# Another order of the mixer's steps, later memory rows and smaller output chunks in a two-layer encoder kernel

## The chip, the core and the metric

The kernel runs on one core of a Trainium2 chip. The metric is the device time of one execution in microseconds. The runs shown before the change have a median of 2234.5 us (three runs, 2233.97 to 2236.01).

## The reference, cut to what matters

```python
for l in range(2):                                   # x: 256 tokens x 2048, mem: 256 x 2048
    h = rms_norm(x, norm_mix[l])
    g_q, g_k, g_v, g_r, lr_f, lr_b, d_q, d_k, d_v, m_q = split(h @ w_in[l])
    gla = head_norm(gla_fwd + gla_bwd) * silu(g_r)   # gated linear attention, 4 heads
    dil = head_norm(dilated_attention(d_q, d_k, d_v) + relative bias)
    kv  = rms_norm(mem, mem_norm[l]) @ w_mem_kv[l]
    xat = head_norm(softmax(m_q @ km) @ vm)          # memory attention
    x = x + concat(gla, dil, xat) @ w_out[l]
    x = x + square(relu(rms_norm(x, norm_mlp[l]) @ w_up[l])) @ w_down[l]
return rms_norm(x, norm_final)                       # all float32
```

## The kernel before, in words

**Products.** Every weight product goes through `linear` (L192). It makes a 256 x 512 result (two token tiles of 128 x 512 in PSUM, pool `ps_mm`, four buffers, so two products at a time) out of four *quads* of 512 weight rows. A quad's 1 MB is loaded by SyncE (SP) into one of three `raw` buffers (`load_quad`, L182). Both operands are split in a high and a low part: ScalarE (ACT) casts `raw` to `wh` (L203), VectorE (DVE) subtracts to get `wl` (L204, "the cut"), in halves of 512 KB, with four buffers each for `wh` and `wl`, which is two quads. Then TensorE (PE) does 24 matmuls (L221 to L223): 4 slices x 2 token tiles x 3 part products. In a product's last quad they are sorted by token tile. `col(i)` is the product of the normalised input with the i-th 512 columns of `w_in`; `evac` (L228) scales a result and moves it from PSUM into SBUF.

**Two lists of other work.** `turning` holds generators that transpose a 256 x 512 activation on DVE with 16 instructions of 32 x 256 (`turn_blocks`, L102) and then, for `split_turned` (L147), make its high and low parts on ACT and DVE. A tuple such as `(0, 4, 4, 4, 4)` says how many of the 16 each step issues; the step after the tuple makes the parts. `turn(n)` (L162) takes n steps of the first generator in the list, `turn()` empties the list. `linear` calls `turn(1)` once per quad behind the cut. `pending` holds functions of which `linear` calls one per quad (`flush(1)`) behind the quad's matmuls. If a quad needs an input that is not ready, `linear` runs steps of the lists until it is.

**Order.** The program text gives the order of priority; the tile framework (called with `schedule_with_timeline_sim=True`, L802) puts the instructions of each engine in a fixed queue and gives out buffers. `with tc.issue_after(ins)` puts those instructions of the block that run on the engine of `ins` behind it in its queue. Most activations live in one pool, `ring`, of 22 slots of 4 KB per partition (`slot`, L54).

**Start.** Transposed memory (`in_memT`) and the first three quads of `w_mem` are loaded in pieces. Then come two small constants, the four 512 KB chunks of plain memory rows into `x` (L528) and the identity. The memory rows serve only for the memory's row norms: `memory_squares` (L568) squares a chunk on ACT and then loads the input rows over it on GpSimd's (POOL) queue. The steps made by `plan_loads` (L531) load the transposed input `xT` during the values product.

**The mixer of a layer** (from L555): memory keys and values (`w_mem`), column 9 (memory queries `mq`), column 0 (`gq`), column 1 (`gk`), memory attention (`attend_weights` L278, `attend_out` L313), the gates (`log_gates`, L343, 14 slots of the ring; its last result is `gl`), columns 2 and 3 (`gv`), all steps up to `gkT` (L612), the gated-attention weights (`gla_weights`, L395), column 6 (`dq`), the gated output (`gla_out`, L472), column 7 (`dk`), column 4 with its silu gate (`gated(0)`), all turning steps (L633), the dilated attention's weights (L634), column 8 (`dv`), its output, column 5, and then `w_out` in four groups, each with the quads 3, 0, 2, 1 (memory, gated, dilated, gated).

**End.** The last `w_down` group's result is added to `x`, squared with a row sum, and the row norm `rs` made of four partial sums (DVE reduce, two POOL instructions, L79 and L81). Then per token tile two halves of 128 x 1024 are scaled on ACT and DVE (L700 to L706) and stored, 512 KB each (L708).

## Time and profile before

| | |
|---|---|
| median of three runs | 2234.5 us |
| the profiled execution's own time | 2234.38 us |
| its span, first to last instruction | 2232.6 us |
| PE busy | 2195.7 us (98%) |
| DVE busy | 1593.3 us (71%) |
| ACT busy | 1133.5 us (51%) |
| POOL busy | 39.7 us (2%) |
| moved by DMA | 423.27 MB, mean 190 GB/s |
| mean granted clock of PE | 0.996 of 2.4 GHz |

The span is what the profile's times count from; the execution's own time is 1.8 us more, for what lies around it. A row of the timeline gives start and duration in us, engine and line, the operation, result and sources by the program's names, how many instructions were merged in it (x16), and in brackets the idle time of the engine before it with what ended it. The engine names with a q are the queues that issue DMAs.

### The profile page before, as it was taken

The numbers are of one execution on the slowest core, as the hardware profiler recorded it, in microseconds if no ns is written. First come the engines' busy times: TensorE is split into PE (matmuls) and PEld (weight loads), VectorE is DVE, ScalarE is ACT, GpSimd is POOL, SyncE is SP. The second block draws the span as 40 slices with busy tenths as digits, with TensorE's granted clock in tenths as the row PEclk, the third lists the DMA queues.
The fourth block names the chain that finished last, engine by engine and source line by source line (L and its number), as shares of the span: only waits on it lengthen the run. The fifth ranks groups of instructions, "written<-read, shape, count | busy, mean of one in ns | idle before, by whom it ended". The sixth has DMA issues, their size and how long they took to land.

```text
span 2232.6 us, 25769 instructions
## 1 busy us (share of the span) xinstructions
PE 2195.7 (98%) x9898; PEld 1818.4 (81%) x9898; DVE 1593.3 (71%) x2234; ACT 1133.5 (51%) x1529; POOL 39.7 (2%) x69
## 2 busy tenths in 40 slices
PE   7998999999999999999999999999999999999998
PEld 5886888888888888888888878888888888888886
DVE  5658688977577477468986588888765864865774
ACT  7555465554355345345554565655544544543543
POOL 1000000000000000000000000000000000000000
PEclk9999999999999999999999999999999999999999
DMA  9653345555555555555665443555555555555563
GB/s 359 226 172 130 132 151 188 189 192 203 189 190 196 198 188 192 197 196 200 215 202 194 154 158 130 181 189 189 192 202 191 190 194 199 189 189 197 195 211 132
DMA packets 63364, 423.27 MB, mean 190 GB/s; under 512 B 7076, under 2 KB 7844, under 8 KB 14473
## 3 DMA queue, kind: packets, MB, share of 16 engines
q1 hardware_dynamic: 62104, 417.69, 54.6%
q0 software_dynamic: 1136, 3.94, 0.5%
q8 instruction: 77, 1.26, 0.2%
q14 instruction: 47, 0.38, 0.0%
HBM read 419.50 MB, written 3.15 MB: 189 GB/s over the span
## 4 chain that ended last, share of the span: by engine, by line
PE 94%; DVE 2%; DMA 2%; ACT 1%; issue 1%; SPq 0%; POOL 0%; ACTq 0%; POOLq 0%; DVEq 0%
PE mm L222 30%; PE mm L223 30%; PE mm L221 30%; DMA raw<-in_w_mem 1%; PE pv L323 1%; PE go L479 1%; DVE gkT L108 1%; DVE wl L204 0%; PE pT L309 0%; DVE gqT L108 0%; DMA x<-in_mem 0%; DVE dkT0o L108 0%; PE dg L439 0%; ACT junk L93 0%; PE dg L443 0%
## 5 line engine op out<-in xcount | busy, mean ns | idle before, releaser
L204 DVE TENSOR_TENSOR wl<-raw,wh 128x1024 fp32r<-128x1024 f32 (+1 forms) x774 | 928.4, 1215 | 533.0 <-ACT wh L203 528.5
L203 ACT ACTIVATE wh<-raw 128x1024 fp32r<-128x1024 f32 (+1 forms) x774 | 813.6, 1054 | 882.1 <-PE mm L223 824.4
L222 PE MATMUL mm<-wl,uT3h 128*128 128x512 f32 x256 | 99.6, 389 | 0.0
L223 PE MATMUL mm<-wh,uT3h 128*128 128x512 f32 x256 | 99.6, 389 | 0.0
L223 PE MATMUL mm<-wh,zT0h 128*128 128x512 f32 x256 | 99.6, 389 | 0.0
L223 PE MATMUL mm<-wh,uT1h 128*128 128x512 f32 x256 | 99.6, 389 | 0.0
L223 PE MATMUL mm<-wh,zT3h 128*128 128x512 f32 x256 | 99.6, 389 | 0.0
L222 PE MATMUL mm<-wl,zT1h 128*128 128x512 f32 x256 | 99.6, 389 | 0.0
L222 PE MATMUL mm<-wl,uT2h 128*128 128x512 f32 x256 | 99.6, 389 | 0.0
L222 PE MATMUL mm<-wl,zT0h 128*128 128x512 f32 x256 | 99.6, 389 | 0.0
L222 PE MATMUL mm<-wl,uT0h 128*128 128x512 f32 x256 | 99.6, 389 | 0.0
L223 PE MATMUL mm<-wh,uT2h 128*128 128x512 f32 x256 | 99.6, 389 | 0.0
L223 PE MATMUL mm<-wh,uT0h 128*128 128x512 f32 x256 | 99.6, 389 | 0.0
L222 PE MATMUL mm<-wl,uT1h 128*128 128x512 f32 x256 | 99.6, 389 | 0.0
L222 PE MATMUL mm<-wl,zT2h 128*128 128x512 f32 x256 | 99.6, 389 | 0.0
L221 PE MATMUL mm<-wh,zT0l 128*128 128x512 f32 x256 | 99.6, 389 | 0.0
L223 PE MATMUL mm<-wh,zT2h 128*128 128x512 f32 x256 | 99.6, 389 | 0.0
L222 PE MATMUL mm<-wl,zT3h 128*128 128x512 f32 x256 | 99.6, 389 | 0.0
L223 PE MATMUL mm<-wh,zT1h 128*128 128x512 f32 x256 | 99.6, 389 | 0.0
L221 PE MATMUL mm<-wh,uT1l 128*128 128x512 f32 x256 | 99.4, 389 | 0.0
L221 PE MATMUL mm<-wh,zT1l 128*128 128x512 f32 x256 | 99.4, 389 | 0.0
L221 PE MATMUL mm<-wh,uT3l 128*128 128x512 f32 x256 | 99.3, 389 | 0.0
(438 smaller groups left out, 4671.6 us busy)
## 6 DMA issues: line engine op xcount, KB each, us to landing
raw<-in_w_up SPq DMA_DIRECT2D x128, 1024.0 KB, 4.9
raw<-in_w_down SPq DMA_DIRECT2D x128, 1024.0 KB, 4.9
raw<-in_w_in SPq DMA_DIRECT2D x80, 1024.0 KB, 4.9
raw<-in_w_out SPq DMA_DIRECT2D x32, 1024.0 KB, 4.9
raw<-in_w_mem SPq DMA_DIRECT2D x13, 1024.0 KB, 5.5
mem<-in_memT SPq DMA_DIRECT2D x7, 512.0 KB, 6.3
raw<-in_w_mem SPq DMA_DIRECT2D x12, 256.0 KB, 6.0
x<-in_mem SPq DMA_DIRECT2D x4, 512.0 KB, 7.0
```

The source lines that it names most:

```text
L108: yield nc.vector.transpose(dst[f:f + 32, :, :, s:s + 32], src[s:s + 32, :, :, f:f + 32])
L203: nc.scalar.activation(hi, raw[:, k:k + n], AF.Copy)
L204: cut = nc.vector.tensor_tensor(lo, raw[:, k:k + n], hi.bitcast(F32), ALU.subtract)
L221: nc.tensor.matmul(ps[t], xl[:, kk, sl], hi, start=first, stop=False)
L222: nc.tensor.matmul(ps[t], xh[:, kk, sl], lo, start=False, stop=False)
L223: nc.tensor.matmul(ps[t], xh[:, kk, sl], hi, start=False, stop=last)
L323: nc.tensor.matmul(ps[:, h, :], pT[s][:, h, t * P:(t + 1) * P], v[:, s, h * P:(h + 1) * P], start=s == 0, stop=s == NT - 1,)
L479: nc.tensor.matmul(ps[:, j, :], AT[s][:, t, 2 * c + j, :], v[c][:, s, j * DV:(j + 1) * DV], start=s == 0, stop=s == NT - 1,)
```

## The change

Five things are done.

- `linear` gets `late`: the matmuls of the last `late` quads are issued together behind the last one, sorted by token tile. It is 2 for the last `w_down` group of the last layer and 1 elsewhere. What `turn(1)` and `flush(1)` issue on ACT is now put behind the quad's last cast too.
- The memory rows are no longer loaded behind the first weights; `plan_loads` loads one chunk per quad of the values product (`load_rows`).
- The mixer's order: memory attention moves behind column 2 in layer 0 and stays behind column 1 in layer 1; the gates move behind column 2; in layer 1 three turning steps run before column 1; `dq`, `dk` and `mT0` are turned in steps of four with an empty first one; the dilated attention moves behind column 8; `turn()` before it becomes steps until `dk` is ready. The line that appends the turn of `gq` stands twice afterwards: the first is a context line of the diff, the second is added.
- The last group is not added to `x` in the loop but per token tile at the end, and the first three partial sums are reduced ahead of the fourth.
- The output is stored in eight chunks of 256 KB, in the order 0, 3, 2, 1 within a token tile.

```diff
--- before.py
+++ after.py
@@ -189,10 +189,11 @@
             newest[0] = nc.sync.dma_start(raw[:, c * n:(c + 1) * n], wsrc[:, k:k + n, :]).ins
         return raw, pieces
 
-    def linear(wsrc, lhs, quads, loaded=(), pool=ps_mm, tag="mm"):
+    def linear(wsrc, lhs, quads, loaded=(), pool=ps_mm, tag="mm", late=1):
         ps = [pool.tile([P, NW], F32, tag=tag, name=f"mm{t}") for t in range(NT)]
-        nq = len(quads)
+        nq, order = len(quads), []
         for i, q in enumerate(quads):
             raw, n = loaded[i] if i < len(loaded) else load_quad(wsrc, q)
             wh = [wpool.tile([P, 2, NW], F32R, tag="wh", name="wh", bufs=4) for _ in range(2)]
@@ -200,28 +201,31 @@
             n = min(4 // n, 2)
             for k in range(0, 4, n):
                 hi, lo = (w[k // 2][:, k % 2:k % 2 + n] for w in (wh, wl))
-                nc.scalar.activation(hi, raw[:, k:k + n], AF.Copy)
+                cast = nc.scalar.activation(hi, raw[:, k:k + n], AF.Copy)
                 cut = nc.vector.tensor_tensor(lo, raw[:, k:k + n], hi.bitcast(F32), ALU.subtract)
-            with tc.issue_after(cut.ins):
+            with tc.issue_after(cut.ins), tc.issue_after(cast.ins):
                 turn(1)
             while q not in lhs:
                 if pending:
                     flush(1)
                 else:
                     turn(1)
-            xh, xl = lhs[q]
-            order = [(kk, t) for kk in range(4) for t in range(NT)]
+            order += [(i, q, wh, wl, kk, t) for kk in range(4) for t in range(NT)]
+            if nq - late <= i < nq - 1:
+                continue
             if i == nq - 1:
-                order.sort(key=lambda o: o[1])
-            for kk, t in order:
+                order.sort(key=lambda o: o[5])
+            for j, p, wh, wl, kk, t in order:
+                xh, xl = lhs[p]
                 sl = slice(t * P, (t + 1) * P)
-                first = i == 0 and kk == 0
-                last = i == nq - 1 and kk == 3
+                first = j == 0 and kk == 0
+                last = j == nq - 1 and kk == 3
                 hi, lo = wh[kk // 2][:, kk % 2, :], wl[kk // 2][:, kk % 2, :]
                 nc.tensor.matmul(ps[t], xl[:, kk, sl], hi, start=first, stop=False)
                 nc.tensor.matmul(ps[t], xh[:, kk, sl], lo, start=False, stop=False)
                 nc.tensor.matmul(ps[t], xh[:, kk, sl], hi, start=False, stop=last)
-            with tc.issue_after(cut.ins):
+            order = []
+            with tc.issue_after(cut.ins), tc.issue_after(cast.ins):
                 flush(1)
         return ps
 
@@ -524,14 +528,18 @@
     nc.sync.dma_start(rel, a["rel"])
     nc.sync.dma_start(onehot, a["onehot"])
     with tc.issue_after(newest[0]):
-        for c in range(4):
+        nc.sync.dma_start(ident, a["ident"])
+
+    def load_rows(c):
+        with tc.issue_after(newest[0]):
             nc.sync.dma_start(x[:, :, c * NW:(c + 1) * NW], tokens(a["mem"], c))
-        nc.sync.dma_start(ident, a["ident"])
-
-    def plan_loads(name, loads, src, gain, lhs):
+
+    def plan_loads(name, loads, src, gain, lhs, also=None):
 
 
         def step(i):
+            if also is not None and i < 4:
+                also(i)
             for q in loads[i] if i < len(loads) else ():
                 splits[name, q] = split_loaded(
                     slot([4, S], f"{name}{q}"), src, q, gain, f"{name}{q}", lhs
@@ -560,7 +568,7 @@
         if l == 0:
             flush()
             bias_products()
-            plan_loads("x0", ((0, 1), (2,), (3,)), a["xT"], gains[:, 0, 0, :], xlhs)
+            plan_loads("x0", ((0, 1), (2,), (3,)), a["xT"], gains[:, 0, 0, :], xlhs, load_rows)
             ps_v = linear(a["w_mem"][l, 1], mem_lhs, range(4), pool=ps_ax, tag="ax")
             with tc.issue_after(newest[0]):
                 spread_bias()
@@ -598,25 +606,35 @@
             queries_turned()
             gq = evac(col(0), rsq, "gq")
         turning.append(heads_turned(gq, "gqT", heads))
-        ps_gk = col(1)
-        while "mq" not in heads:
-            turn(1)
-        o_mem = attend_out(attend_weights(heads["mq"], heads["km"], None, "mem"), vm, "memo")
-        gk = evac(ps_gk, rs, "gk")
-        gates = log_gates(xlhs, rs, l)
-        turning.append(heads_turned(gk, "gkT", heads))
         mlhs = {}
         mgain = gains[:, 1, l, :]
-        turning.append(split_turned(o_mem, 3, mgain, "mT3", mlhs, (0, 4, 4, 4, 4)))
-        gv = [evac(col(2 + c), rs, f"gv{c}") for c in range(2)]
+
+        def memory_attention():
+            while "mq" not in heads:
+                turn(1)
+            o = attend_out(attend_weights(heads["mq"], heads["km"], None, "mem"), vm, "memo")
+            turning.append(heads_turned(gk, "gkT", heads))
+            turning.append(split_turned(o, 3, mgain, "mT3", mlhs, (0, 4, 4, 4, 4)))
+
+        turning.append(heads_turned(gq, "gqT", heads))
+        if l:
+            turn(3)
+        gk = evac(col(1), rs, "gk")
+        if l:
+            memory_attention()
+        gv = [evac(col(2), rs, "gv0")]
+        if not l:
+            memory_attention()
+        gates = log_gates(xlhs, rs, l)
+        gv.append(evac(col(3), rs, "gv1"))
         while "gkT" not in heads:
             turn(1)
         AT = gla_weights(heads["gqT"], heads["gkT"], gates)
         dq = evac(col(6), rsq, "dq")
         o_gla = gla_out(AT, gv)
-        turning.append(split_turned(dq, "dq", None, f"dqT{l}", heads, (0, 8, 8)))
+        turning.append(split_turned(dq, "dq", None, f"dqT{l}", heads, (0, 4, 4, 4, 4)))
         dk = evac(col(7), rs, "dk")
-        turning.append(split_turned(dk, "dk", None, f"dkT{l}", heads, (0, 8, 8)))
+        turning.append(split_turned(dk, "dk", None, f"dkT{l}", heads, (0, 4, 4, 4, 4)))
 
         def gated(c):
             ps = col(4 + c)
@@ -630,11 +648,11 @@
             mlhs[1] = split_T(o_gla[1], 1, mgain, "mT1")
 
         gated(0)
-        turn()
-        weights = attend_weights(heads["dq"], heads["dk"], bt, "dil")
-        turning.append(split_turned(o_gla[0], 0, mgain, "mT0", mlhs, (4, 4, 4, 4)))
+        turning.append(split_turned(o_gla[0], 0, mgain, "mT0", mlhs, (0, 4, 4, 4, 4)))
         dv = evac(col(8), rs, "dv")
-        o_dil = attend_out(weights, dv, "dilo")
+        while "dk" not in heads:
+            turn(1)
+        o_dil = attend_out(attend_weights(heads["dq"], heads["dk"], bt, "dil"), dv, "dilo")
         turning.append(split_turned(o_dil, 2, mgain, "mT2", mlhs, (0, 4, 4, 4, 4)))
         gated(1)
         pending.append(mixed)
@@ -676,7 +694,10 @@
                     plan_loads(
                         "mem1", ((0,), (1,), (2,), (3,)), a["memT"], gains[:, 3, l + 1, :], mem_lhs
                     )
-                ps = linear(a["w_down"][l, part, g], ulhs, range(up_groups))
+                ending = end and last and g == 3
+                ps = linear(a["w_down"][l, part, g], ulhs, range(up_groups), late=2 if ending else 1)
+                if ending:
+                    continue
                 add_to_x(ps, g)
                 if end and not last:
                     pending.append(lambda g=g: squares_of_x(xnorm, g))
@@ -691,21 +712,25 @@
     out_rows = a["out"].rearrange("(t p) d -> p t d", p=P)
     for t in range(NT):
         v = xchunk(3, t)
+        part = small.tile([P, 1], F32, tag="part", name="part")
+        nc.vector.tensor_reduce(part, fnorm.ssc[:, t, :3], AX.X, ALU.add)
+        nc.gpsimd.tensor_scalar(part, part, 1.0 / D, EPS, ALU.mult, ALU.add)
+        nc.vector.tensor_tensor(v, ps[t], v, ALU.add)
         fnorm.add(3, t, v)
-        rs = fnorm.done(t)
-        for half in (1, 0):
-            for c in (2 * half, 2 * half + 1):
-                v = xchunk(c, t)
-                if c == 3:
-                    nc.vector.scalar_tensor_tensor(
-                        v, v, rs[:, 0:1], fg[1][:, 1, :], ALU.mult, ALU.mult
-                    )
-                elif c == 1:
-                    nc.vector.tensor_scalar(v, v, rs[:, 0:1], None, ALU.mult)
-                else:
-                    nc.scalar.activation(v, v, AF.Copy, scale=rs[:, 0:1])
-            cs = slice(2 * half * NW, (2 * half + 2) * NW)
-            nc.sync.dma_start(out_rows[:, t, cs], x[:, t, cs])
+        m = small.tile([P, 1], F32, tag="m1", name="m_fin")
+        nc.gpsimd.tensor_scalar(m, fnorm.ssc[:, t, 3:], 1.0 / D, part[:, 0:1], ALU.mult, ALU.add)
+        rs = small.tile([P, 1], F32, tag="rs_fin", name="r_fin")
+        nc.gpsimd.tensor_tensor(rs, m, neghalf[:, :1], ALU.pow)
+        for c in (0, 3, 2, 1):
+            v = xchunk(c, t)
+            cs = slice(c * NW, (c + 1) * NW)
+            if c == 3:
+                nc.vector.scalar_tensor_tensor(v, v, rs[:, 0:1], fg[1][:, 1, :], ALU.mult, ALU.mult)
+            elif c == 1:
+                nc.vector.tensor_scalar(v, v, rs[:, 0:1], None, ALU.mult)
+            else:
+                nc.scalar.activation(v, v, AF.Copy, scale=rs[:, 0:1])
+            nc.sync.dma_start(out_rows[:, t, cs], v)
 
 
 def _bucket(rel):
```

## Rows read from the trace of the kernel before

**Rows 1.** The page's first section: busy time, share of the span, instructions per engine

```profile
PE 2195.7 (98%) x9898; PEld 1818.4 (81%) x9898; DVE 1593.3 (71%) x2234; ACT 1133.5 (51%) x1529; POOL 39.7 (2%) x69
```

**Rows 2.** Waits of PE: us in total, times, longest us

```profile
PE mm L222 <- DVE wl L204: 16.3, 6, 9.7
PE mm L221 <- ACT wh L203: 11.0, 4, 5.5
```

**Rows 3.** Stretches: length, each engine's busy time, granted clock, DMA share, GB/s

```profile
10.00:64.50 54.50, 46.72 (x185) 35.24 (x184) 32.16 (x54) 40.07 (x84) 8.54 (x14) 0.97 0.99 374
188.60:207.00 18.40, 8.72 (x35) 6.97 (x34) 17.89 (x37) 6.33 (x17) 0.52 (x1) 0.72 0.18 61
540.00:1080.00 540.00, 540.00 (x2384) 447.16 (x2383) 360.72 (x464) 256.38 (x274) 0.00 (x0) 1.00 0.57 197
```

**Rows 4.** Timeline of SP's DMA issues and of PE, the start

```profile
15.03 2.40 SPq L528 DMA_DIRECT2D x<-in_mem  x4
...
29.10 0.73 PE L221 MATMUL mm<-wh,mem03l 128*128 128x512 f32 x2 [2.53 <-ACT wh L203]
...
64.51 0.61 PE L221 MATMUL mm<-wh,x00l 128*128 128x512 f32 x2
```

**Rows 5.** Timeline of DVE and PE in layer 0, behind the gates

```profile
185.30 1.22 DVE L392 TENSOR_TENSOR gl<-z,gh 128x1024 fp32r<-128x1024 f32 x1
186.44 7.18 DVE L108 STREAM_TRANSPOSE gqT<-gq 32x256 f32<-32x256 f32 x16
193.65 7.20 DVE L108 STREAM_TRANSPOSE gkT<-gk 32x256 f32<-32x256 f32 x16
...
202.76 0.80 PE L222 MATMUL mm<-wl,x00h 128*128 128x512 f32 x1 [9.68 <-DVE wl L204]
```

**Rows 6.** Timeline of ACT, DVE and PE in layer 1, behind the gates

```profile
1292.39 1.24 ACT L231 ACTIVATE gv<-mm,r_mix 128x512 f32<-128x512 f32 x2
1293.65 7.18 DVE L108 STREAM_TRANSPOSE gkT<-gk 32x256 f32<-32x256 f32 x16
...
1302.14 0.50 PE L222 MATMUL mm<-wl,xT0h 128*128 128x512 f32 x1 [1.84 <-DVE wl L204]
```

**Rows 7.** Timeline, layer 0: PE begins columns 7 and 4, evictions between

```profile
226.71 0.39 PE L221 MATMUL mm<-wh,x00l 128*128 128x512 f32 x1
...
237.28 1.28 ACT L231 ACTIVATE dq<-mm,rsq 128x512 f32<-128x512 f32 x2
238.03 0.69 DVE L426 TENSOR_TENSOR qd<-gqT,E 128x512 f32<-128x512 f32 x1
...
255.94 0.39 PE L221 MATMUL mm<-wh,x00l 128*128 128x512 f32 x1
...
280.89 1.25 ACT L231 ACTIVATE dk<-mm,r_mix 128x512 f32<-128x512 f32 x2
```

**Rows 8.** Timeline of PE in layer 0, column 8's first quad

```profile
292.29 0.50 PE L222 MATMUL mm<-wl,x00h 128*128 128x512 f32 x1 [2.74 <-DVE wl L204]
```

**Rows 9.** Timeline of PE and DVE in layer 0: memory attention, third `w_out` quad

```profile
130.47 0.28 PE L236 MATMUL sc<-kmT0h,mqT0l 128*128 128x256 f32 x1
...
158.16 0.67 DVE L337 TENSOR_TENSOR memo<-pv,cmb 128x512 f32<-128x512 f32 x1
...
354.22 1.66 DVE L128 SCALAR_TENSOR_TENSOR mT2l<-mT2o,gains,mT2h 128x256 fp32r<-128x256 f32 x4
...
355.67 0.39 PE L221 MATMUL mm<-wh,mT2l 128*128 128x512 f32 x1
```

**Rows 10.** End: timeline of DVE, SP; DMA issues (KB each, us to landing)

```profile
2220.53 0.69 DVE L502 TENSOR_TENSOR x<-mm,x 128x512 f32<-128x512 f32 x1 [5.84 <-PE mm L223]
...
2224.18 0.68 DVE L502 TENSOR_TENSOR x<-mm,x 128x512 f32<-128x512 f32 x1
...
2223.94 4.57 SPq L708 DMA_DIRECT2D out<-x  x4
...
out<-x SPq DMA_DIRECT2D x4, 512.0 KB, 3.1
```

## The prediction, made before the changed kernel was run

> **What bounds the kernel now.** The page's first section comes first: TensorE (PE) is busy 98% of a span of 2232.6 us, the matmul count is not touched by the change, so all that can be won is PE's idle time, some 37 us, and stretches at the lower clock [rows 1]. Next, PE's waits: in total it waits 16.3 us for VectorE's (DVE) `wl` cuts and 11.0 us for ScalarE's (ACT) `wh` casts; the rest of the idle time is the first 5.5 us and the tail behind the last matmul [rows 2]. Then busy time by stretches: 10 to 64.5 us has PE busy for 46.7 of 54.5 us with the DMA engines at 0.99, 188.6 to 207 us has it busy for 8.7 of 18.4 us at a granted clock of 0.72 with DVE busy for 17.9 us; 540 to 1080 us is unbroken, 2384 matmuls in 540 us, that is 0.2265 us each and 5.44 us for a quad's 24 [rows 3]. So: DMA at the start, DVE in the mixer of layer 0, and a serial tail.
>
> **Part 1, memory rows later.** The four 512 KB loads of memory rows are issued at 15.03 us, ahead of the last `w_mem` quad of the keys; that quad's matmuls end an idle time of 2.53 us at 29.10 us [rows 4]. From the start of that idle time (26.57 us) to the first matmul of column 9 (64.51 us) PE has five quads, 27.2 us of work, and takes 37.9 us: 10.7 us are lost, in six waits for the next weights and in the slower matmuls behind them [rows 3, 4]. The change issues one memory chunk behind each value quad. Everything column 9's first quad needs by then is 2 MB memT, 8 MB weights, 2 MB rows, 2 MB xT and 1 MB of its own; at the stretch's 374 GB/s [rows 3] that is 40 us, and PE reaches it at 53.6 us at best, so the order, not the volume, is what starves PE. The x loads on the GpSimd queue, which now run against the weights since they follow the memory squares, also move behind. What becomes late: the squares of memory and x stand behind a cast in each quad of columns 9 and 0, and casts run at most two quads ahead of PE, so the last squares come near 66 and 88 us and the row norms some 2 us behind them. The evictions that wait for the norms (keys, query) free the PSUM pairs of columns 0 and 1, which PE wants near 53.6 + 4 x 5.44 = 75 and 97 us: 5 us of cover; if that goes, PE waits by the difference. Bounds: all 10.7 us, or half, 5 us, if the weight ring of three raw buffers keeps loads as close as now. I take **-10.0 us**, near the upper end, since PE waits nowhere in 540 us at 197 GB/s, half the start's rate [rows 3].
>
> **Part 2, mixer order.** I counted each transposing step. A `turn(1)` runs per weight quad. The diff appends the turn of `gq` a second time and leaves the first in place, so 16 more DVE transposes (16 take 7.2 us [rows 5]) per layer. More important is the ring of 22 slots. In layer 1 `gkT` starts at 1293.65 us, straight behind the last `gl`, and `gv`, whose matmuls were long done, at 1292.39 us [rows 6]; in layer 0 `gqT` and then `gkT` start only behind the last `gl` (185.30 us) [rows 5]. I read this as slots given out in program order: whatever is traced after the gates waits for the gates' last slot. With the change, layer 0's second `gqT` and `gkT` are still both traced after the gates, so the burst of 32 transposes, 14.4 us, stays, and with it PE's 9.68 us of waiting; layer 1's `gkT` burst of 16 with its 1.84 us stays too [rows 5, 6]. I take **0** (bounds: 7.8 us saved, if only 16 are left as in layer 1; 3 us lost, if the doubled work comes on top). The duplicate itself runs in DVE's gaps.
>
> What moves is the cover. Layer 0's memory attention starts one column later, so one column fewer is left to run beside the gate weights (`gla_weights`). Column 4 needs the PSUM pair of column 6, which the eviction of `dq` frees; that waits in slot order for the second `qd` (238.03 us) and ends at 238.56 us. Column 7's pair is freed by `dk` at 282.14 us, after the gated output [rows 7]. Today column 6 ends near 226.7 us, column 4 starts at 255.9 and column 8 near 289, so neither matters [rows 7, 8]; afterwards column 7 ends where column 6 does in the chain, and PE waits. If the chain were no faster, the waits are 238.6-226.7 less some 3.6 us of chain work, 8 us, and about 11 us more before column 8: 19 us. But PE's queue is then empty of columns, so each chain step starts when ready; with the 4 to 5 us by which the chain's matmuls now stand behind columns taken off, I get 2.5 to 3 us at each place: **+5.2 us** (bounds 0 and 19). The second stall of now, 2.74 us up to 292.29 us for `wl`, goes, since the bunches of eight transposes of `dq` and `dk` before it become fours, spread to the end of column 8: **-2.7 us** [rows 8].
>
> Dilated attention is now traced behind column 8, so column 5 and two `w_out` quads are its whole cover, 10.9 us + 21.8 us + some 10 us of its own and `mT1`'s PE work: 43 us. Its transposed output `mT2`, five turns of which now stand in one row before `w_out`'s third quad, needs the attention (28 us for the memory group, 130.47 to 158.8 us [rows 9]), 7.2 us of transposes, 1.7 us of parts, and what DVE does for others. Today its parts start at 354.22 us, the last of the four ending at 355.88, against a first use at 355.67 us: no slack; layer 1 repeats the pattern [rows 9]. Bounds 0 and 10 us a layer; I take 1.5 us, near the lower, as the transposes may fill DVE's gaps: **+3.0 us**. In layer 1 the gates' loads now stand behind `gv0`'s slot, some 9 us later; `dk` there has about that slack: **+0.4 us**. Putting ACT's parts and squares behind the casts costs nothing in the unbroken stretch: ACT is busy 256 of 540 us there [rows 3].
>
> **Part 3, the tail.** Sorting the last two quads by token tile ends tile 0's sum 2.7 us sooner (12 matmuls). Now tile 0's sum is added at 2220.53 us, tile 1's at 2224.18 us instead of 2.7 us later, because DVE is at tile 0's scalings until then [rows 10]; those 0.9 us go. The reduce of four partial sums (0.16 us and its hand-over) leaves the chain, and the first store needs one scaled chunk rather than two, 0.7 us. Against it stand four more DMA issues of some 0.34 us on SP, of which two lie behind the first store. The stores are then bound by 1 MB at the rate of now (2 MB in four stores, 3.1 us to landing each [rows 10]). I take **-1.4 us** (bounds -2.4 and 0). The Trainium skill, "DMA: Bandwidth & Descriptors", speaks against this step: its section Bandwidth wants transfers of 1 MiB or more, and the fit in "Anatomy of one DMA" (made on transfers issued from GpSimd) has about 2 us of fixed cost in each, an estimate of 2.6 us for 256 KB. By that, four in turn would take 10.4 us against 6.4 us for two of 512 KB. No row here shows them in turn.
>
> **Sum:** -10.0 + 0 + 5.2 - 2.7 + 3.0 + 0.4 - 1.4 = -5.5 us, on the profiled execution's own 2234.38 us (span 2232.6): 2228.9; the median of the runs is 0.1 higher, so **2229.0 us**.
>
> **Rivals.** (a) The mixer gives nothing back: slots are freed early enough, columns never wait for PSUM, `mT2` fits in. For it: the chain steps now stand behind columns. Against: `dq` and `dk` ended exactly in slot order. Time: 2234.5 - 10.0 - 1.4 - 2.7 = 2220.4 us; were the burst halved too, 2212. (b) **Slower:** the PSUM pairs come no earlier than now. Place: columns 4 and 8 of layer 0; price 19 us instead of 5.2, so 2229.0 + 13.8 = 2242.8 us; it decides once `dq` and `dk` gain less than about 4 us each on the chain. For it: evictions and chain are planned beforehand, on estimated times. Against: the planner sees the empty PE. (c) The start gain is not there: with the ring of three raw buffers the rows only move the queue, 5 us instead of 10, hence 2234.0 us, no change. (d) Stores in turn at 3.1 us each instead of overlapping: 6.2 us more than two, 2236.6 us. Against it: the four stores of now are all issued within 4.57 us, overlapping [rows 10]. The Trainium skill's rule above is what would have it so.
>
> **Chances.** Forecast (2225 to 2234) 0.44; (a) 0.22; (b) 0.20; (c) 0.11; (d) 0.03. A measurement of this kernel tells some 0.2%, 4.5 us, from no change. Faster by more: all of (a), 0.6 of the forecast: 0.48. Slower by more: (b) and a rest: 0.22. Within: 0.30. The range takes in most of (a) and (b): 2219 to 2242 us; the forecast's own is 2225 to 2234.
>
> **What would show it.** Start: the first column 9 matmul near 54 us and no wait before it but the first. Burst: 32 transposes in a row behind the last `gl` of layer 0, again. PSUM: two waits of PE of 2 to 4 us, ended by ACT's `dq` and `dk`, and none at the 292 us place. `w_out`: at most 2 us before its third quad in each layer. Tail: tile 1's add within 0.1 us of PE's end, and 8 us from there to the span's end. I am wrong if columns wait longer than 10 us in all in layer 0, if `gqT` and `gkT` are not together behind the gates, or if the start's waits remain.

## The result, and the profile after

The changed kernel takes 2262.65 us (median of four runs, 2257.66 to 2264.41) against 2234.23 us: ratio 1.0119, 95% interval 1.0102 to 1.0136. It is 28.4 us slower, outside the range, and on the other side of the forecast. The profiled execution took 2264.41 us (span 2262.5).

The page's first section answers to [rows 1]: the same 9898 matmuls, PE busy 9.6 us longer although nothing was added to it, and 32 more DVE instructions (16 transposes a layer).

```profile
span 2262.5 us, 25817 instructions
PE 2205.3 (97%) x9898; PEld 1825.8 (81%) x9898; DVE 1608.7 (71%) x2266; ACT 1135.0 (50%) x1529; POOL 41.8 (2%) x71
```

PE's waits after answer to [rows 2]; the columns are the waiting engine and line, the releaser, us in total, times, longest.

```profile
PE mm L224 <- DVE mT0l L128: 18.1, 2, 9.0
PE mm L225 <- DVE wl L205: 13.9, 2, 11.4
PE mm L224 <- ACT wh L204: 6.5, 2, 5.1
PE mm L224 <- ACT dk L235: 5.2, 2, 3.1
PE mm L224 <- DVE mem01l L128: 1.8, 1, 1.8
PE mm L224 <- ACT dq L235: 1.3, 1, 1.3
```

Of the start's waits for `wh` only the first, of 5.1 us, is left (the other in that row, 1.4 us, is in layer 1). New are two waits of 9 us for `mT0l`, one in each layer's `w_out`, and those for `dk` and `dq`. A ledger of the first matmul of each stage, before and after (us from the start of the span), says where the time went:

| first matmul of | before | after | shift | won (-) or lost since the row above |
|---|---|---|---|---|
| column 9, layer 0 | 64.5 | 55.5 | -9.0 | -9.0 |
| `w_out`, layer 0 | 343.9 | 340.7 | -3.1 | +5.9 |
| `w_up`, layer 0 | 431.8 | 442.4 | +10.6 | +13.7 |
| `w_out`, layer 1 | 1438.8 | 1455.4 | +16.6 | +6.0 |
| `w_up`, layer 1 | 1526.7 | 1556.2 | +29.5 | +12.8 |
| end of the span | 2232.6 | 2262.5 | +29.9 | +0.4 |

So the start gave what was forecast, the tail nothing, and each layer lost about 19 us between column 9 and `w_up`. Three places of layer 0 in the timeline show it. First DVE behind the gates (start, duration, engine, line, operation, and in brackets the idle time before with its releaser), which answers to [rows 5]:

```profile
202.32 2.36 DVE L396 TENSOR_TENSOR gl<-z,gh 128x1024 fp32r<-128x1024 f32 x2
204.60 7.18 DVE L108 STREAM_TRANSPOSE gqT<-gq 32x256 f32<-32x256 f32 x16
211.81 7.20 DVE L108 STREAM_TRANSPOSE gkT<-gk 32x256 f32<-32x256 f32 x16
219.04 0.69 DVE L430 TENSOR_TENSOR qd<-gqT,E 128x512 f32<-128x512 f32 x1
```

Against column 9's start, `gl`'s second instruction begins at 148.0 us instead of 120.8, and the burst of 32 is still whole. Then PE's four longest waits in this layer's mixer:

```profile
220.92 0.80 PE L225 MATMUL mm<-wl,x01h 128*128 128x512 f32 x1 [11.43 <-DVE wl L205]
247.23 0.50 PE L224 MATMUL mm<-wh,x00l 128*128 128x512 f32 x1 [1.33 <-ACT dq L235]
288.95 0.80 PE L224 MATMUL mm<-wh,x00l 128*128 128x512 f32 x1 [3.15 <-ACT dk L235]
357.94 0.80 PE L224 MATMUL mm<-wh,mT0l 128*128 128x512 f32 x1 [9.03 <-DVE mT0l L128]
```

And DVE ahead of the last of them, which answers to [rows 9]:

```profile
348.17 0.69 DVE L341 TENSOR_TENSOR dilo<-pv,cmb 128x512 f32<-128x512 f32 x1
348.89 3.12 DVE L108 STREAM_TRANSPOSE mT2o<-dilo 32x256 f32<-32x256 f32 x7
...
355.64 1.34 DVE L108 STREAM_TRANSPOSE mT2o<-dilo 32x256 f32<-32x256 f32 x3
357.01 0.48 DVE L128 SCALAR_TENSOR_TENSOR mT1l<-mT1ps,gains,mT1h 128x256 fp32r<-128x256 f32 x1
357.41 1.66 DVE L128 SCALAR_TENSOR_TENSOR mT0l<-mT0o,gains,mT0h 128x256 fp32r<-128x256 f32 x4
359.11 0.89 DVE L108 STREAM_TRANSPOSE mT2o<-dilo 32x256 f32<-32x256 f32 x2
360.03 0.88 DVE L128 SCALAR_TENSOR_TENSOR mT1l<-mT1ps,gains,mT1h 128x256 fp32r<-128x256 f32 x2
360.82 1.66 DVE L128 SCALAR_TENSOR_TENSOR mT2l<-mT2o,gains,mT2h 128x256 fp32r<-128x256 f32 x4
```

PE waits for `mT0l`, and `mT0l` stands on DVE's queue behind 14 of `mT2`'s transposes. That row invites a theory, and the theory is wrong, as the next section shows. The clock is told by the windows (columns: stretch, length, PE busy and count, granted clock, DMA share, GB/s):

```profile
240.00:245.90 5.90, 5.90 (x34) 1.00 0.53 182
247.20:251.80 4.60, 4.57 (x13) 0.63 0.29 123
251.80:257.00 5.20, 5.20 (x30) 1.00 0.00 0
289.00:293.50 4.50, 4.50 (x14) 0.66 0.02 4
357.94:366.41 8.47, 8.46 (x25) 0.66 0.00 0
366.41:371.90 5.49, 5.49 (x26) 1.00 0.39 122
```

Behind each of these waits the matmuls run partly at the lower level: 24 of them take 8.5 us instead of 5.5 behind the wait of 9.03 us, and 12 take 4.4 and 4.3 us instead of 2.7 behind the two short ones. That is why PE is busier with the count unchanged.

PE's own time closes the account. From column 9 to the `w_up` of layer 1 it takes 38.5 us more (1500.7 instead of 1462.2): it is idle for 26.2 us more (40.5 instead of 14.3) and busy for 12.3 us more with the same 6633 matmuls.

### The profile page after: what moved, and what is told of

The parts are those of the page before. It is cut to its first block, busy times and chain, and to the rows that moved or that the text cites. A ratio compares the mean times of both kernels' runs of the same rounds, so it can differ in the third digit from the quotient of the medians.

```text
span 2262.5 us, 25817 instructions
## 1 busy us (share of the span) xinstructions
PE 2205.3 (97%) x9898; PEld 1825.8 (81%) x9898; DVE 1608.7 (71%) x2266; ACT 1135.0 (50%) x1529; POOL 41.8 (2%) x71
## 3 DMA queue, kind: packets, MB, share of 16 engines
HBM read 419.50 MB, written 3.15 MB: 187 GB/s over the span
## 4 chain that ended last, share of the span: by engine, by line
PE 85%; DVE 2%; ACT 1%; issue 0%; POOL 0%; ACTq 0%; POOLq 0%; DVEq 0%
PE mm L224 28%; PE mm L225 27%; PE mm L226 27%; PE go L483 1%; DVE mT2o L108 1%; DVE wl L205 0%; ACT wh L204 0%; PE pv L327 0%; DVE gkT L108 0%; ACT junk L334 0%; PE pT L313 0%; PE dg L447 0%; PE dg L450 0%; PE xg L470 0%; PE cum L412 0%
```

## The experiments

Every kernel was timed against the kernel before on the same chip. For all of them distances were read in both layers, to and from the start of `dk`'s second eviction (us; "mT2" is the start of the last of its four low parts). The marks are those of the profiled execution; that of e4 took 2258.8 us, 5.4 us more than its median.

| kernel | median | ratio | col. 9 to dk | dk to mT2 | dk to `w_up` | layer 1: `w_up` of layer 0 to dk | dk to `w_up` |
|---|---|---|---|---|---|---|---|
| before | 2234.2 | 1 | 217.0 | 73.9 | 150.3 | 942.2 | 152.7 |
| after | 2262.7 | 1.0119 | 233.3 | 73.2 | 153.6 | 960.9 | 152.9 |
| e1 rows only | 2225.2 | 0.9954 | 217.0 | 74.6 | 151.4 | 942.1 | 152.8 |
| e2 one turn | 2245.0 | 1.0042 | 225.5 | 73.2 | 153.5 | 950.1 | 153.3 |
| e3 mT0 by eights | 2263.5 | 1.0126 | 233.9 | 76.9 | 155.4 | 961.9 | 151.8 |
| e4 attention before col. 8 | 2253.4 | 1.0087 | 233.3 | 74.0 | 151.2 | 962.0 | 148.8 |
| e5 memory attention early | 2253.9 | 1.0085 | 227.7 | 71.7 | 150.7 | 961.8 | 150.8 |
| e6 gates early | 2258.5 | 1.0101 | 228.0 | 73.3 | 153.7 | 952.5 | 164.1 |
| e7 rows and forced tail | 2225.0 | 0.9953 | 216.0 | 74.6 | 151.4 | 942.1 | 152.8 |
| e8 gates early, one turn | 2238.9 | 1.0014 | 215.2 | 73.4 | 152.4 | 945.4 | 164.0 |
| e9 turned before gates | 2230.9 | 0.9976 | 218.0 | 73.3 | 151.4 | 944.8 | 154.1 |
| e10 gates first | 2222.8 | 0.9940 | 218.5 | 72.5 | 148.2 | 944.0 | 151.2 |
| e11 gates, then memory | 2228.6 | 0.9968 | 214.8 | 72.3 | 149.1 | 953.9 | 149.1 |
| e12 three undone | 2230.4 | 0.9982 | 217.9 | 72.5 | 150.4 | 950.1 | 149.3 |
| e13 four undone | 2228.1 | 0.9965 | 214.6 | 74.7 | 151.5 | 944.2 | 154.2 |

The 95% intervals reach 0.0009 to 0.0017 to either side of the ratio.

**The start alone (e1).** The kernel before with `load_rows` and nothing else:

```diff
-        for c in range(4):
-            nc.sync.dma_start(x[:, :, c * NW:(c + 1) * NW], tokens(a["mem"], c))
+    def load_rows(c):
+        with tc.issue_after(newest[0]):
+            nc.sync.dma_start(x[:, :, c * NW:(c + 1) * NW], tokens(a["mem"], c))
...
+            if also is not None and i < 4:
+                also(i)
```

> The kernel before with the later memory rows alone. Theory (the start's gain is real and independent of the rest): column 9's first matmul at 55.5 us as in the changed kernel against 64.5, and the 9.0 us stay to the end, as nothing between there and the end takes up slack: 2234.2 - 9.0 = 2225.2 us, ratio 0.996. Rival (the later squares and x loads are paid for further on, hidden in the changed kernel's other losses): 2229 to 2234 us, with a new wait of PE before column 1 or in the memory attention.

Measured 2225.15 us, ratio 0.9954 (0.9939 to 0.9969). Column 9 starts at 53.8 us, and every later mark keeps the gain (`w_up` of layer 1 1517.1 against 1526.7). The theory holds; so the new mixer lost some 38 us, not 28.

**The doubled turn (e2).** The changed kernel without the first of the two equal lines:

```diff
-        turning.append(heads_turned(gq, "gqT", heads))
```

> The changed kernel without the doubled turn of gq, nothing else. Theory (the bursts behind the gates are what the doubled turn causes): layer 0 has 16 transposes (7.2 us) behind the last gl instead of 32, so PE's 11.4 us wait falls to about 4 us; in layer 1 gkT gets the steps of columns 1 and 2, the 16 behind gl vanish and with them waits of 1.4 and 2.4 us and some slow matmuls. Together 9 to 13 us less than the changed kernel: 2250 to 2254 us. The two waits of 9.0 us before w_out's second quad stay. Rival (the doubled work runs in gaps and the chain behind gl sets the end anyway): 0 to 3 us less, 2260 to 2263 us.

Measured 2244.97 us, 17.7 less than the change as it was, more than expected: the largest single part. In layer 0 the burst is 16 and PE's wait 3.6 us: `gkT` begins straight behind `gl`, at 203.34 us, where as changed (rows above) the second `gqT` stands between them with its 7.2 us.

```profile
203.34 7.17 DVE L108 STREAM_TRANSPOSE gkT<-gk 32x256 f32<-32x256 f32 x16
```

In layer 1 these are DVE's rows, with the one turn and, below them, as changed:

```profile
1257.47 3.56 DVE L108 STREAM_TRANSPOSE gkT<-gk 32x256 f32<-32x256 f32 x8
1262.32 1.79 DVE L108 STREAM_TRANSPOSE gkT<-gk 32x256 f32<-32x256 f32 x4
1267.20 1.80 DVE L108 STREAM_TRANSPOSE gkT<-gk 32x256 f32<-32x256 f32 x4
1303.64 1.23 DVE L396 TENSOR_TENSOR gl<-z,gh 128x1024 fp32r<-128x1024 f32 x1
```

```profile
1266.66 5.36 DVE L108 STREAM_TRANSPOSE gqT<-gq 32x256 f32<-32x256 f32 x12
1273.31 1.79 DVE L108 STREAM_TRANSPOSE gqT<-gq 32x256 f32<-32x256 f32 x4
...
1316.66 1.22 DVE L396 TENSOR_TENSOR gl<-z,gh 128x1024 fp32r<-128x1024 f32 x1
1317.80 7.19 DVE L108 STREAM_TRANSPOSE gkT<-gk 32x256 f32<-32x256 f32 x16
```

There the second turn of `gq` does not cost its 7.2 us of DVE; it takes the steps of the list that `gkT` would have had, and so `gkT` falls behind the gates, where it is in the way. Without it, `gkT` is done 35 us ahead of `gl`. So the duplicate costs its own duration in layer 0 (`dk` 7.9 us later) and another's place in layer 1 (`dk` 10.8 us later). The two waits for `mT0l` stay (17.4 us).

**Where the 9 us in `w_out` come from (e3, e4).** I first held DVE's queue to be the cause: that `mT0`'s parts, tied to the second `w_out` quad, are overtaken by `mT2`'s transposes.

```diff
-        turning.append(split_turned(o_gla[0], 0, mgain, "mT0", mlhs, (0, 4, 4, 4, 4)))
+        turning.append(split_turned(o_gla[0], 0, mgain, "mT0", mlhs, (0, 8, 8)))
```

> The changed kernel with mT0 turned in steps (0, 8, 8) instead of (0, 4, 4, 4, 4), so that its parts belong to column 5's last quad and no longer to w_out's second. Theory (DVE's queue: mT0's low parts stand behind 14 of mT2's transposes, only because their step comes behind the second w_out quad's cut): the two waits of 9.0 us before w_out's second quad vanish, the 2 to 3 us of slow matmuls behind each too, 22 us in all: 2240 to 2243 us; before the third quad at most 2 us of wait in each layer. Rival (the late dilated attention is what costs: mT2 is ready only when it is, and the wait moves to the third quad): waits of 5 to 9 us before w_out's third quad instead, 2255 to 2263 us.

```diff
+        turn()
+        weights = attend_weights(heads["dq"], heads["dk"], bt, "dil")
+        turning.append(split_turned(o_gla[0], 0, mgain, "mT0", mlhs, (4, 4, 4, 4)))
         dv = evac(col(8), rs, "dv")
-        while "dk" not in heads:
-            turn(1)
-        o_dil = attend_out(attend_weights(heads["dq"], heads["dk"], bt, "dil"), dv, "dilo")
+        o_dil = attend_out(weights, dv, "dilo")
```

> The changed kernel with the weights of the dilated attention back before column 8, all steps emptied ahead of it and mT0 in steps (4, 4, 4, 4), as in the kernel before. Theory (DVE's queue): the waits of 9.0 us in w_out vanish as in the run with mT0 by eights, and column 8 has its cover back: 2238 to 2243 us. Rival (late dilated attention): also 2238 to 2243 us here, but only here and not in the run with mT0 by eights. Third possibility (the reordered columns 6, 7, 4 keep costing in some other place): above 2246 us.

With `mT0` by eights, 2263.54 us: nothing won. `mT0l` is ready at 346.9 us, and PE waits one quad later, for `mT2l`. PE's and DVE's rows of that run:

```profile
352.25 0.69 DVE L341 TENSOR_TENSOR dilo<-pv,cmb 128x512 f32<-128x512 f32 x1
353.99 7.17 DVE L108 STREAM_TRANSPOSE mT2o<-dilo 32x256 f32<-32x256 f32 x16
363.12 1.66 DVE L128 SCALAR_TENSOR_TENSOR mT2l<-mT2o,gains,mT2h 128x256 fp32r<-128x256 f32 x4
363.65 0.79 PE L224 MATMUL mm<-wh,mT2l 128*128 128x512 f32 x1 [10.47 <-DVE mT2l L128]
```

My theory fell; the rival had it right that the wait only moves. But the rival's own cause does not hold either: with the attention back ahead of column 8 (2253.43 us, 9.2 less) the long waits in `w_out` go, yet `mT2` is no earlier, its last part starting 74.0 us behind `dk` (73.2 as changed), and `dk` still comes at 233.3 us. The third possibility, above 2246 us, is what happened. In layer 0 of all fifteen kernels `mT2` follows `dk` by 71.7 to 76.9 us and `w_up` follows it by 148 to 155 us. By these marks 35.0 of the 38.5 us lie ahead of `dk`, 16.3 in layer 0 and 18.7 in layer 1; the long waits behind it are where much of that shows.

That distance is no law, though. In the changed order column 8 starts 0.2 us behind `dk`, whose PSUM pair it waits for, and the attention starts some 3 us into column 5 (26.7 us behind `dk`) and takes 33.4 us. With the attention ahead of column 8 it starts 13.0 us behind `dk` and takes 45.3 us beside the column: the two differences nearly cancel. In the kernel before, PE is busy for 147.6 of the 150.4 us from `dk` to `w_up`, so there PE's own work fills the distance; in the changed kernel it is busy for 144.4 of 153.6 us and waits.

**What makes `dk` late (e5, e6, e8).** Layer 0's memory attention back behind column 1; the gates ahead of column 2; and the latter with one turn:

```diff
-        if l:
-            memory_attention()
+        memory_attention()
         gv = [evac(col(2), rs, "gv0")]
-        if not l:
-            memory_attention()
```

```diff
+        gates = log_gates(xlhs, rs, l)
         gv = [evac(col(2), rs, "gv0")]
         if not l:
             memory_attention()
-        gates = log_gates(xlhs, rs, l)
```

> The changed kernel with layer 0's memory attention back behind column 1 (as layer 1 has it); gates still behind column 2, the doubled turn of gq stays. New theory (one serial chain from the gates' last gl over gkT, gla_weights, dq, dk and the dilated attention to mT2 sets layer 0's end; the change starts it 26 us later against the columns): gl at 175 to 182 us instead of 203.5, mT2's last part some 20 us earlier, layer 0's 9.0 us wait in w_out gone with its slow matmuls (11.9 us) and most of the PSUM waits for dq and dk (4.5 us and 3 us of slow matmuls); layer 1 as in the changed kernel, still with its 9.0 us: 2242 to 2248 us. Rival (dilated attention behind column 8 and steps of four are what makes mT2 late, wherever the gates stand): layer 0's wait in w_out stays above 5 us, 2254 to 2262 us.

> The changed kernel with the gates ahead of column 2 instead of behind it, in both layers; everything else, the doubled turn too, stays. Serial-chain theory: in layer 0 the chain then starts with gkT behind the memory attention (172 us) instead of with gl at 203.5, in layer 1 with gl some 10 us or more earlier; both 9.0 us waits in w_out shrink below 3 us, and the PSUM waits shrink: 2230 to 2242 us. Rival (late dilated attention): both waits stay above 5 us: 2250 to 2262 us.

> The changed kernel with the gates ahead of column 2 and without the doubled turn of gq. Serial-chain theory: beside the gates' gain the burst in layer 0 is 16 transposes instead of 32, so the chain starts another 7 us earlier and PE's wait there is below 5 us: 2222 to 2232 us. If the two faults do not add up (the burst falls beside columns by then), the same as the run with early gates alone, within 3 us.

Measured 2253.94, 2258.45 and 2238.89 us: 8.7, 4.2 and 23.8 less than the change. All three missed the theory's forecast, and the waits in `w_out` stayed at 9.0 us in layer 0 in all three, which is what the rival had said for the first two. So that part of the theory was wrong: those waits do not measure the loss. `dk` comes nearer to it: it came 5 to 6 us earlier against column 9 in the first two and 18 us in the third, which gains more than the sum of its two parts (4.2 + 17.7 us). In the run with early gates `gl` was there at 155 us, but `gkT`, whose turn is appended behind the memory attention, ended its burst at 202 us, as late as with early memory attention. The chain needs both, and the later one counts.

In layer 1 the runs with early gates have 164 us from `dk` to `w_up` instead of 153. There `dk` comes before PE needs it: column 8 starts 12.5 and 14.3 us behind `dk`, and the attention, which this order puts behind column 8, starts 37.2 and 36.1 us behind `dk` instead of 26.6. So an earlier `dk` is worth nothing where the attention waits for the column: of the 8.5 us that it came earlier in the run with early gates, 11.2 were lost again behind it.

**The other way round (e9, e10, e11).** If a later chain costs, does an earlier one gain? On the kernel before with later rows, `gq` and `gk` are turned ahead of the gates (e9), the gates come ahead of the memory attention, which then follows column 2 (e10) or comes right behind the gates (e11). What e10 adds, without the lines that it takes away; e11 is without its `gv` line, and e9 keeps `o_mem` first:

```diff
+        gk = evac(ps_gk, rs, "gk")
+        turning.append(heads_turned(gk, "gkT", heads))
+        while "gkT" not in heads:
+            turn(1)
+        gates = log_gates(xlhs, rs, l)
+        gv = [evac(col(2), rs, "gv0")]
         o_mem = attend_out(attend_weights(heads["mq"], heads["km"], None, "mem"), vm, "memo")
```

> The kernel before with the later memory rows, and with gq and gk turned (steps run out in the program) ahead of the gates instead of behind them; all else as before. Serial-chain theory (what counts is when gkT and gl are both there, since dk follows 70 to 81 us later, and mT2 72 to 77 us after dk, in every run so far): gkT is done before gl (175 to 180 us), so the chain starts 11 to 15 us earlier in layer 0 and 7 in layer 1, PE's wait of 9.7 us behind the gates falls below 2 us and the slow matmuls behind it go; w_out's third quad still finds mT2 ready. 2225.2 - 9 to 13 us: 2212 to 2216 us. Rival (the 32 transposes only move ahead of the gates on DVE and delay gl by the same 14 us): gl at 185 us or later, 2222 to 2227 us.

> As the run with gq and gk turned before the gates, and the memory attention put behind column 2, after the gates, in both layers (its result is wanted only by w_out's first quad). Serial-chain theory: gl near 150 us, dk some 25 us earlier than in the kernel before, so that from the gates on PE is never short of work for this chain: no wait above 2 us in either mixer, 2209 to 2215 us. Rival (memory attention becomes the new chain, as in the changed kernel, or holds ring slots that gla_weights wants): a wait before gla_weights or w_out of 5 us or more, 2218 to 2230 us.

> As the run with the gates first, but the memory attention right behind the gates, ahead of column 2, in both layers. Serial-chain theory: gl near 150 us, the memory attention then competes with gla_weights for ScalarE and VectorE, dk 10 to 20 us earlier than before: 2210 to 2217 us. Rival (memory attention ahead of gla_weights in the order costs its whole 28 us again): waits as before, 2220 to 2228 us.

Measured 2230.86, 2222.84 and 2228.64 us against 2225.15 with the rows alone. All three forecasts (2209 to 2217 us) missed. In the first the transposes only moved ahead and held `gl` back to 192 us instead of 175, as its rival said; at 2230.86 us it is slower than the rival's 2222 to 2227 too. In the second `gl` is there at 166 us, the 9.7 us wait behind the gates is gone (4.8 us for the gates' own weights is new), and PE is busy 99% of the span; but `dk` still comes 218.5 us behind column 9. PE is busy for 212.1 of these, so little idle time was left to win. It is not that `dk` waits for its own column: column 7 ends at 243.5 us in that run, and `dk` is evicted at 271.62 us, behind the gated output's last squares on ACT (270.22 us). From the end of `gl` to `dk` the chain now takes 106 us, against 94 with the rows alone, beside columns that PE has in the meantime; what stretches it was not separated. An earlier chain therefore gains next to nothing here. The run with the gates first is the fastest of all (ratio 0.9940, 0.9923 to 0.9956); from the rows alone (0.9954, 0.9939 to 0.9969) it is not told apart. These two are faster than the kernel before and the changed one.

**The tail (e7).** The kernel before with later rows, the changed tail, and the second token tile's matmuls tied behind the first tile's last one (the part of the edit that does this):

```diff
+                with ExitStack() as behind:
+                    if late > 1 and t and i == nq - 1:
+                        behind.enter_context(tc.issue_after(ended))
```

> The kernel before with the later memory rows and the change's whole tail, and with the second token tile's matmuls of the last two quads put behind the first tile's on TensorE's queue, so that the planner cannot interleave them. Against the run with the later rows alone (2225.2 us). Theory (the tail's reason holds, only the order was lost): tile 0's add 5.4 us before PE's end, its scalings and stores done while tile 1 still multiplies, tile 1's add within 0.3 us of PE's end, and 7.5 to 8 us from there to the span's end, against 9.2 of before: 1 to 2 us less, 2223 to 2224.5 us. Rival (eight stores of 256 KB cost what the order gives): 2225 to 2227 us, with the last store landing more than 3.5 us behind its issue.

Measured 2224.96 us, the same as the rows alone (2225.15), and between the theory's 2223 to 2224.5 us and the rival's 2225 to 2227. Rows of that run, from DVE, POOL and PE's last matmul:

```profile
2208.80 0.69 DVE L713 TENSOR_TENSOR x<-mm,x 128x512 f32<-128x512 f32 x1 [3.12 <-PE mm L229]
2213.82 0.39 PE L229 MATMUL mm<-wh,uT3h 128*128 128x512 f32 x1
2214.24 0.69 DVE L713 TENSOR_TENSOR x<-mm,x 128x512 f32<-128x512 f32 x1 [1.73 <-PE mm L229]
2215.86 0.27 POOL L716 TENSOR_SCALAR m_fin<-ssc_fin,part 128x1 f32<-128x1 f32 x1 [4.53 <-ACT junk L93]
2216.80 0.75 DVE L723 SCALAR_TENSOR_TENSOR x<-x,r_fin,fg 128x512 f32<-128x512 f32 x1 [1.86 <-POOL r_fin L718]
```

The order now holds: the first tile's add comes 5.4 us before PE's end, the second's 0.03 us behind it. From PE's end (2214.21) to the span's end it is still 9.1 us, against 9.4 with the rows alone (last matmul 2213.19 plus 0.39, span 2223.0). The DMA rows of the last 19 us say where the rest went, eight stores of 256 KB here and four of 512 KB with the rows alone (GB/s in 40 slices):

```profile
GB/s 0 0 0 0 0 0 0 0 0 0 0 0 0 0 0 0 91 371 392 362 362 384 246 0 0 0 0 0 302 388 384 375 345 354 60 0 0 0 0 0
```

```profile
GB/s 0 0 0 0 0 0 0 0 0 0 0 0 0 0 0 0 0 0 0 0 0 259 405 423 405 405 311 0 0 362 405 397 414 414 216 0 0 0 0 0
```

The small stores run side by side, not in turn, but in the last group at 345 to 388 GB/s instead of 397 to 414 (whole slices). Its first store is issued 3.3 us behind PE's end instead of 4.4, so the order gives 1.1 us; its last one is issued 1.4 us behind the first instead of 0.5, and by the span's end 0.3 us of the gain is left. The number of issues and the rate were not tried apart. The Trainium skill ("DMA: Bandwidth & Descriptors", Bandwidth) asks for larger transfers, by a table made on loads that GpSimd issued; the direction agrees here on stores, by about a tenth of the rate.

**Closing the account (e12, e13).** One turn, early memory attention and the attention before column 8 together (the edits above), and in the second the gates also ahead of column 2:

> The changed kernel without the doubled turn of gq, with layer 0's memory attention behind column 1, and with the dilated attention ahead of column 8 (mT0 in steps (4, 4, 4, 4)); the gates still behind column 2, dq and dk still in fours, rows, casts and tail as changed. If the parts are independent, 2262.6 - 17.7 - 8.7 - 9.1 = 2227 us. If they hide behind the same late chain (each helps only until PE, not the chain, sets dk), less: 2231 to 2240 us. dk's eviction relative to column 9's first matmul: 217 to 219 us in the kernel before and in all kernels without waits; 233 in the changed kernel; the nearer to 217, the more of layer 0 is back.

> As the run with three parts undone, with the gates also back ahead of column 2 (behind the memory attention). What remains of the change beside the rows and the tail are the steps of four for dq and dk and the order of parts behind casts. If these are harmless: 2225 to 2227 us, within 0.1% of the kernel before with later rows; dk 217 us behind column 9's first matmul and, in layer 1, 942 us behind the first w_up matmul of layer 0. If the steps of four for dq and dk cost by themselves (dk's parts come two columns later): 2229 us or more.

Measured 2230.36 and 2228.05 us. Three parts together give 32.3 us, where the sum of the single runs is 35.6, so they overlap a little (the forecasts had 2227 us for no overlap and 2231 to 2240 for much); with the gates 34.6. `dk` is back at 214.6 us in layer 0 and at 944.2 in layer 1. What is left of the change, the steps of four, the casts and the tail, is 2.9 us above the rows alone, within what the intervals of the two leave open, and between the forecast for harmless steps of four (2225 to 2227 us) and that for costly ones (2229 or more): whether they cost anything stays open. The account: -9.1 (rows) + 34.6 (doubled turn, late memory attention, late gates, late dilated attention) + 2.9 = +28.4 us.

## Why the prediction was wrong

**Start, -10.0: right.** -9.0 us by the marks, and 0.9954 alone. (Its 15 MB are 15.7 million bytes, so 42 us at 374 GB/s and not 40; nothing hangs on it.)

**The burst, "I take 0": wrong, and by the runs the largest miss.** That 32 transposes would stand behind `gl` was right, to the row. "The duplicate itself runs in DVE's gaps" was the failed step. In layer 0 its 16 transposes stand in the chain, between `gl` and `gkT`, so that the 7.8 us that the stated bound had for a burst of 16 were not saved; in layer 1 it uses up steps that were `gkT`'s. Undoing it gives 17.7 us, 7.9 of `dk` in layer 0 and 10.8 in layer 1.

**PSUM, +5.2: the waits right, the reason wrong.** PE does wait for `dq` (1.33 us) and `dk` (3.15 us), 4.5 us. But I expected the pairs to come earlier on the chain, and against column 9 they came 18.1 and 16.3 us later, for `gl` came 27 us later. In the new order column 8, and the attention behind it, start only behind `dk`, and the sum had no term for that. I had 19 us as the upper bound and as rival (b); I set it aside on the ground that the planner sees an empty PE. What I should have weighed was the place of the gates.

**The 2.74 us stall, gone: right**, though a wait for `dk` stands at column 8 instead.

**`w_out`, +3.0: failed by size, and by PE's waits the largest term.** From the first score matmul (315.5 us) the attention took 33.4 us where I had 28 from the memory group; from there to the end of `mT2`'s parts it was 13.6 us instead of 8.9. That is 47.0 us; the cover was 38.9 (to 354.4, where the third quad would have begun) instead of 43. PE waited 9.0 us in each layer, 18.1 in all. That `mT0l`, on DVE's queue behind `mT2`'s transposes, was the cause fell with e3.

**Slow matmuls: left out.** No term of the sum had the matmuls behind a new wait: 3.0 us behind the 9 us wait of layer 0 and 2.0 behind that of layer 1, 1.7 and 1.6 behind layer 0's waits for `dq` and `dk`; 12.3 us in all between column 9 and layer 1's `w_up`.

**Layer 1, +0.4: wrong.** The failed step is that `dk` "has about that slack". Against the first `w_up`, `gl` came 13.6 us later where I had some 9, `gkT`'s burst of 16 stood behind it as before, and `dk` came 18.7 us later: there was no slack. Ahead of `dk` PE waited 4.0 us more than before.

**Tail, -1.4: wrong, 0.4 lost.** The step that failed was the order: the planner interleaved the two tiles, and the second add again stood behind the first tile's scalings. Forced (e7), the order gives what I said, the stores take back most of it, and the whole is 0.2 us, which is no difference.

By PE's own waits the 26.2 us are +1.8 at the burst, +4.5 for `dq` and `dk`, -2.7 for the stall, +18.1 in `w_out`, +4.0 in layer 1 and 0.7 for a `gv` that no term had.

Of the rivals, (b) had the sign. Its condition held, for the PSUM pairs came no earlier; but at its places PE waited 4.5 us and not 19, and its 2242.8 us are 20 us short, so its sign is partly luck. (d) did not happen: stores overlap, 2.7 us each to landing.

## What to carry to other kernels

A wait says who was late last, not where the time was lost: measure the distances between fixed marks of the serial chain (here gates, `dk`, `mT2`, the next product), and look for the first one that grew. In a scheme where work is handed out by steps, the price of an extra piece of work is set by its place: in layer 0 it stood in the chain with its whole duration, in layer 1 it took the steps of a piece that the chain needed. Before moving a step behind other work, ask which chain it starts, and how long that chain is; here moving the gates' end 27 us later made `dk` 16 us later, while moving it earlier gained almost nothing, with PE then busy for nearly all of the time.

## What the runs showed of the hardware that I had not expected

A short wait can cost more than itself. In the changed kernel, an idle time of 1.33 us at 247.23 us was followed by 4.6 us at a granted clock of 0.63, that is partly at 1.2 instead of 2.4 GHz, though the clock had been at 1.00 up to 245.9 us; the last 3.8 us of work ahead of it were matmuls of 64 and 320 columns. In the run with the gates first, idle times of 1.07 us (up to 127.06 us) and 1.59 us (up to 344.09 us), both behind matmuls of 512 columns, were followed by stretches at 1.00:

```profile
127.00:130.00 3.00, 2.94 (x12) 1.00 0.41 164
344.10:349.80 5.70, 5.70 (x25) 1.00 0.63 227
```

The Trainium skill ("TensorE: Matmul & The Clock Gate", HAM oscillation) tells of waits after which the next work runs at half the clock; the 9 us wait agrees with it (0.66), and for the short ones these rows show both outcomes. What decides between them was not tried.
